# Layer 0's adaLN modulation as column-quarter products on TensorE

## The chip, the cores and the metric

One core of a Trainium2 chip runs the kernel. Its engines are TensorE (PE, with its weight loads listed as PEld), VectorE (DVE), ScalarE (ACT), GpSimd (POOL) and SyncE (SP), whose queue issues the large loads. Each has an instruction stream of its own, in a fixed order; semaphores make one wait for another. The metric is the device time of the kernel in microseconds, lower is better. "Span" is the time from the first to the last instruction of one profiled execution.

## The reference

A sequence of 256 tokens with 1024 features goes through a first block (gated delta rule and dilated attention side by side, then a convolved, gated FFN) and a second block of two layers (attention and a mixture of 16 experts), whose norms are modulated by a row computed from a conditioning vector `c`:

```python
x = x + jnp.concatenate([y_a, y_b], axis=-1) @ w_out     # first block: mix
x = x + (silu(conv(h @ w_gate)) * (h @ w_up)) @ w_down   # first block: FFN
for i in range(2):                                       # second block
    mod = silu(c) @ ada_w[i] + ada_b[i]                  # [1, 1024] @ [1024, 6144]
    sh1, sc1, g1, sh2, sc2, g2 = split(mod, 6)
    x = x + g1 * mixer(rms_norm(x) * (1 + sc1) + sh1)
    x = x + g2 * moe(rms_norm(x) * (1 + sc2) + sh2)
```

The change touches `mod` for i = 0, which depends on `c` alone. It is computed while the first block runs, long before layer 0 needs it.

## The kernel before

All weights are streamed once from HBM through SBUF, mostly in units of 1 MB ([128, 2048] fp32), issued by SP into a ring of rooms (`w`, four of them; the modulation's units into `wa`, two rooms). Large products with 256 tokens split each fp32 operand into a high and a low half (`wh`, `wl`; `hh`, `hl`; `yh`, `yl`) and make three products of them (lines L543 and L559 to L561); a split is a cast on ACT and a subtraction on DVE, or on POOL for a part of the units (L232). PSUM has two rings of four tiles, tag `pa` for the projections and `pb` for everything else; a projection to token rows (`tok`) holds two `pa` tiles while its products add up, the output projection (`mix`) one for each token block and half of the columns.

The first block runs in these stages: features of the delta rule (L543, `pa`), convolved on DVE (L798); decay factors and heads (L835 to L903); the inverse of a triangular matrix by doubling (levels: two products on 64x64 blocks at L917, then R copied by DVE at L927, then Y and X updated at L933 and L934); joining of the halves (L942, L948); the chunk recurrence (L959); dilated attention (L604 to L627); the output projection (L559 to L561 with `yh`, `yl`); the norm (L441 products that only keep PE busy, L473, transposes L481); and the FFN (L543 with `pb`).

The second block's modulation is worked in between. `ada(n)` issues the next n units, with fractions carried; 48 units make both layers. In the delta rule `fill(n, more)` advances a "filler" (the projections `w_v`, `w_z` and the dilated attention) by n steps and calls `ada(more)` at each; the remaining units are issued in the FFN's loop. A unit, before, is half of the 1024 rows (four blocks of 128) of 512 columns. `ada_unit` multiplies each block of 128 rows by its 128 values of silu(c), one per partition (`csil`), and adds it up in `acc` [128, 512]: three blocks on DVE (L376 for the first of all, L381 for the others), the fourth scaled on ACT (L378) and added on POOL (L379). After two units the column's eight blocks are in `acc`, and `ada_sum` adds up the 128 partitions on PE: four products of `ones` with 128 columns each (L393), on four different parts of 32 columns of the array. For the gates g1 and g2 a product with the identity adds the bias (L396). ACT copies the result (L398) and sends it to a row in DRAM, `adar` (L399), from which the second block reads it.

The program's text gives only a first order: a scheduler with a priority by program order places each instruction where the tiles it needs are free, so it decides where the modulation's instructions stand on each engine.

Of the kernel before, what the change touches and what calls it, by code (L numbers as in the profile page):

```python
# [27 lines left out]
# columns of the packed per-partition parameters  # L28
# [7 lines left out]
# columns of the packed rows that every partition gets  # L36
ROW = {"alog": (0, 4), "dtb": (4, 8), "rb": (8, 24), "lam": (24, 280)}
NROW = 280
# columns of the shape constants
# [7 lines left out]
# the first block needs those up to here  # L47
# [3 lines left out]
def _constants():  # L51
# [23 lines left out]
    # negated bias of the merged dilated attention: [q, head, (previous block | own block) keys back to front]  # L75
# [8 lines left out]
    # one-hot T5 bucket of rel = key - query, for rel = 127 .. -384  # L84
# [9 lines left out]
def _pack(inp):  # L94
# [6 lines left out]
    def feat(w):  # L101
        """[D, n] -> units of two blocks of 128 columns, each [128, k, 128 columns]"""
        n = w.shape[1]
        return A(w.reshape(KD, 128, n // 256, 2, 128).transpose(2, 1, 3, 0, 4)).reshape(n // 256, 128, 2048)

    def tok(w):
        """[D, n] -> units of 512 columns and half the rows, each [128, 4 k, 512 columns]"""
        n = w.shape[1]
        return A(w.reshape(2, 4, 128, n // 512, 512).transpose(3, 0, 2, 1, 4)).reshape(n // 256, 128, 2048)
# [27 lines left out]
    o["ada_w"] = A(g["ada_w_2"].reshape(2, 2, 4, 128, 12, 512).transpose(0, 4, 1, 3, 2, 5)).reshape(48, 128, 2048)  # L137
# [19 lines left out]
class InOrder:  # L157
    """an engine whose instructions keep their order in the program"""
# [10 lines left out]
def tile_block(ctx: ExitStack, tc: tile.TileContext, a: dict, out: bass.AP, dbg=None):  # L169
# [60 lines left out]
    def split(h, l, i, eng=None):  # L230
        """i = h + l exactly, each of a float32r's width"""
# [32 lines left out]
    # the tensor engine's clock rises while x is on its way  # L264
# [25 lines left out]
    def wpair(ap, n):  # L290
        """(e, i) -> the i-th 512 columns of a unit for one of two experts; the n-th unit of a layer also finds room where activations were"""
# [30 lines left out]
    def after(i, name):  # L322
        """i is issued behind an instruction of its engine"""
# [3 lines left out]
    # rooms for split halves: s of two tiles of their own, 8 of one where activations are not  # L327
# [10 lines left out]
    def subs(ap, w=None, pinned=False, by=None, behind=None):  # L338
        """a unit of weights, loaded now or already on its way, as two split halves"""
# [25 lines left out]
    def ada_unit(n):  # L365
        """half the rows (four blocks) of 512 columns of a layer's modulation, every fourth block on GpSimd"""
        l, s, u = n // 24, n // 2 % 12, n % 2
        w = adap.tile([128, 2048], F32, tag="wa", name="wa", bufs=2)
        nc.sync.dma_start(w, a["ada_w"][n])
# [16 lines left out]

    def ada_sum(l, s, acc):
        """sum over partitions; with the bias for the gates, which are used as rows"""
# [16 lines left out]
    def ada(n):  # L405
        """n units more, fractions carried"""
# [12 lines left out]
    def ada_finish(l, t):  # L419
        """shift and scale as columns (the gates, used as rows, have the bias already)"""  # L420
# [15 lines left out]
    def warm(*waits):  # L436
        """holds the tensor engine's clock up through waits; nothing reads the products"""
# [5 lines left out]
    def rsq(o, i, scale):  # L443
        """o = (i * scale + eps) ** -0.5 through the activation tables"""
# [10 lines left out]
    def norm_rows(update=None, column_major=False, between=None, scaled=True):  # L455
        """x after update(b, c) of its [block, half row] pieces, and the rows of x over their root mean square"""
# [19 lines left out]
    def turned(src, column_major=False):  # L476
        """[128 tokens, 2, D] -> (j, [128, 2 blocks of columns from j on, 256 tokens]) in PSUM"""
# [27 lines left out]
    def spread(rs):  # L505
        """[128, 256 tokens]: the factor of each token, on every partition"""
# [7 lines left out]
    def kept(r, n):  # L514
        """r, the clock held up while the first columns are made"""
        warm(*[r[:, 128 * (i % 2):128 * (i % 2) + 16] for i in range(n)])
        return r

    def cols_split(turned_, r, scale, bias):
        """rows turned before their factors r were known, as two split halves"""  # L520
# [16 lines left out]
    def feat(p, h, wh, wl):  # L537
        """p[128 features, 256 tokens]; wh, wl [128, 8 k, 128]"""
# [12 lines left out]
    def tok_half(p, u, h, k, k0=0):  # L551
        """adds blocks k .. k + 3 of the rows, a unit of [128, 4 k, 512], to p[b] [128 tokens, 512]; in two steps"""
# [12 lines left out]
    def tok(units, h, done):  # L565
        """[128 tokens, 512] for both token blocks; four steps, then done(p)"""
# [11 lines left out]
    def weave(*parts):  # L578
        """runs (generator, steps a round) side by side in program order"""
# [10 lines left out]
    def lag(n, *stages):  # L590
        """stage j of item i comes j steps after its first stage"""
# [7 lines left out]
    def scores(qT, kT, blk, half, nbias, pt, den):  # L599
        """pt [128, 384] gets exp(s - max): keys 0..255 of query block 1, then keys 0..127 of query block 0.  # L600
        q comes negated; nbias [128, 256] is the negated bias for the keys of the (previous | own) block, back to front."""
# [13 lines left out]
    def flip(pt):  # L615
        """[q, keys] probabilities -> [keys, 2 blocks, q]"""
# [12 lines left out]
    def plain_heads(h0, n, qT, kT, v, nbias, y):  # L629
        """heads h0 .. h0 + n - 1 of plain attention; y(pair) gives the places of a pair's output"""  # L630
# [24 lines left out]
    # ================= first block =================  # L655
# [69 lines left out]
    n = 0  # L725
# [985 lines left out]
```

## Time and profile before

| | |
|---|---|
| median of the runs shown | 1169.7 us (1168.49 to 1181.19) |
| span of the profiled execution | 1168.8 us |
| PE busy | 1091.2 us, 93% |
| DVE busy | 668.5 us, 57% |
| ACT busy | 467.4 us, 40% |
| POOL busy | 202.3 us, 17% |
| DMA | 349.75 MB, mean 299 GB/s |
| mean granted clock of TensorE | 0.980 of full speed |

The page gives each engine's busy time over the whole span; the windows view gives it for stretches, and the share of a stretch in which PE is not busy is what can be won there. The waits view adds up the idle time of an engine in front of its instructions by what released them. The timeline lists instructions by start, with the idle time before each in brackets. Rows of one kind that follow each other are put together and counted.

### The profile page before, as it was taken

The numbers are of one execution on the slowest core, as the hardware profiler recorded it, in microseconds if no ns is written. First come the engines' busy times: TensorE is split into PE (matmuls) and PEld (weight loads), VectorE is DVE, ScalarE is ACT, GpSimd is POOL, SyncE is SP. The second block draws the span as 40 slices with busy tenths as digits, with TensorE's granted clock in tenths as the row PEclk, the third lists the DMA queues.
The fourth block names the chain that finished last, engine by engine and source line by source line (L and its number), as shares of the span: only waits on it lengthen the run. The fifth ranks groups of instructions, "written<-read, shape, count | busy, mean of one in ns | idle before, by whom it ended". The sixth has DMA issues, their size and how long they took to land. (4 is left out here: it accounts for less than half of the span.)

```text
span 1168.8 us, 16805 instructions
## 1 busy us (share of the span) xinstructions
PE 1091.2 (93%) x6428; PEld 713.0 (61%) x6428; DVE 668.5 (57%) x1283; ACT 467.4 (40%) x942; POOL 202.3 (17%) x156
## 2 busy tenths in 40 slices
PE   8978889899999989999899998898999899999798
PEld 6957677788898868787334434236876544443332
DVE  6999987899999866777322212026656723221212
ACT  5763365655555565667211112016555511110200
POOL 2245543133123242001000000004221100000000
PEclk9999979899999999999999999899999989999999
DMA  8664766777877965356888999998653679899995
GB/s 323 253 252 182 264 246 223 284 285 279 338 284 311 369 247 177 135 200 221 333 349 343 418 422 423 406 421 316 191 184 144 254 305 372 327 424 424 422 419 203
DMA packets 53083, 349.75 MB, mean 299 GB/s; under 512 B 6392, under 2 KB 7192, under 8 KB 13056
## 3 DMA queue, kind: packets, MB, share of 16 engines
q1 hardware_dynamic: 50288, 342.51, 75.2%
q0 software_dynamic: 1792, 5.62, 1.7%
q8 instruction: 55, 0.90, 0.3%
q10 hardware_dynamic: 912, 0.43, 0.1%
q14 instruction: 36, 0.29, 0.1%
HBM read 347.40 MB, written 1.14 MB: 298 GB/s over the span
## 5 line engine op out<-in xcount | busy, mean ns | idle before, releaser
L1544 PE MATMUL pb<-w,XT 128*64 128x512 f32 x864 | 200.1, 609 | 10.3 <-PEq L1504 10.3
L232 DVE TENSOR_TENSOR wl<-w,wh 128x1024 fp32r<-128x1024 f32 x110 | 141.7, 1292 | 40.5 <-ACT wh L232 34.8
L232 ACT CAST wh<-w 128x1024 fp32r<-128x1024 f32 x132 | 137.6, 1044 | 65.5 <-PE pa L560 45.9
L1544 PEld LDWEIGHTS pb<-w,XT 128*64 128x64 f32 x864 | 61.9, 140 | 128.2 <-issue 124.5
L379 POOL TENSOR_TENSOR acc<-acc,wa 128x512 f32<-128x512 f32 x48 | 78.1, 1627 | 204.1 <-DVE acc L381 132.9
L1563 DVE TENSOR_TENSOR he<-he,pb 128x512 f32<-128x512 f32 (+1 forms) x20 | 11.4, 580 | 175.7 <-PE pb L1544 175.7
L381 DVE SCALAR_TENSOR_TENSOR acc<-wa,csil,acc 128x512 f32<-128x512 f32 x120 | 104.0, 867 | 13.4 <-POOL acc L379 8.9
L1581 PE MATMUL pb<-w,heT 128*64 128x512 f32 x480 | 108.1, 597 | 1.5 <-ACT heT L222 1.5
L1562 ACT ACTIVATE he<-pb 128x512 f32<-128x512 f32 (+1 forms) x20 | 10.0, 512 | 209.3 <-PE pb L1544 209.3
L559 PE MATMUL pa<-wh,hh 128*128 128x512 f32 x224 | 91.0, 408 | 2.5 <-ACT hh L532 2.5
L560 PE MATMUL pa<-wh,hl 128*128 128x512 f32 x224 | 88.4, 395 | 3.0 <-POOL hl L530 1.7
L561 PE MATMUL pa<-wl,hh 128*128 128x512 f32 x224 | 88.4, 394 | 0.0
L232 POOL TENSOR_TENSOR wl<-w,wh 128x1024 fp32r<-128x1024 f32 x22 | 54.7, 2488 | 178.3 <-ACT wh L232 139.4
L1584 DVE SCALAR_TENSOR_TENSOR he<-pb,gsl,g 128x512 f32<-128x512 f32 x32 | 24.0, 751 | 96.9 <-PE pb L1581 96.8
L1581 PEld LDWEIGHTS pb<-w,heT 128*64 128x64 f32 x480 | 32.8, 137 | 64.6 <-issue 58.5
L543 PE MATMUL pb<-hh,whl 128*128 128x256 f32 x320 | 62.3, 288 | 0.9 <-DVE gate L1076 0.9
L232 ACT CAST yh<-he 128x512 fp32r<-128x512 f32 x30 | 18.5, 616 | 103.6 <-DVE he L1584 103.6
L378 ACT ACTIVATE wa<-wa,csil 128x512 f32<-128x512 f32 x48 | 34.6, 722 | 58.5 <-DMA wa<-in_ada_w 57.2
L543 PE MATMUL pb<-hh,wh 128*128 128x256 f32 x192 | 55.5, 289 | 1.1 <-DVE hl L236 1.1
L543 PE MATMUL pb<-hl,wh 128*128 128x256 f32 x192 | 55.4, 288 | 0.0
L543 PE MATMUL pb<-hh,wl 128*128 128x256 f32 x192 | 55.2, 288 | 0.0
L543 PEld LDWEIGHTS pb<-hh,whl 128*128 128x128 f32 x320 | 51.3, 192 | 4.0 <-issue 3.4
(455 smaller groups left out, 2352.4 us busy)
## 6 DMA issues: line engine op xcount, KB each, us to landing
w<-in_m_gu SPq DMA_DIRECT2D x108, 1024.0 KB
w<-in_m_dn SPq DMA_DIRECT2D x58, 1024.0 KB
wa<-in_ada_w SPq DMA_DIRECT2D x48, 1024.0 KB
w<-in_w_gu SPq DMA_DIRECT2D x22, 1024.0 KB
w<-in_a_qkv SPq DMA_DIRECT2D x12, 1024.0 KB
wx<-in_m_gu SPq DMA_DIRECT2D x12, 1024.0 KB
w<-in_b_qkv SPq DMA_DIRECT2D x12, 1024.0 KB
w<-in_w_dn SPq DMA_DIRECT2D x11, 1024.0 KB
```

Of the source, the lines that this page charges most:

```text
L232: return A_.copy(h, i), (eng or V).tensor_tensor(l, i, h.bitcast(F32), op=ALU.subtract)
L378: A_.activation(wi, wi, AF.Copy, scale=csil[:, k:k + 1])
L379: G.tensor_tensor(acc, acc, wi, op=ALU.add)
L381: V.scalar_tensor_tensor(acc, wi, csil[:, k:k + 1], acc, op0=ALU.mult, op1=ALU.add)
L543: mm(p, w[:, c], r[:, k, :], start=(n == 0), stop=(n == 3 * KD - 1))
L559: mm(p[b], hh_, wh[:, c], start=(k == k0), stop=False)
L560: mm(p[b], hl_, wh[:, c], start=False, stop=False)
L561: mm(p[b], hh_, wl[:, c], start=False, stop=((k + 1) % KD == k0))
L1544: mm(pu[i][64 * e:64 * e + 64, :], xt[k // 4][:, k % 4, c0 + 64 * e:c0 + 64 * e + 64], w(e, i), start=(k == 0), stop=(k == KD - 1))
L1563: V.tensor_tensor(he[:, cs], he[:, cs], pu[1][:, cs], op=ALU.mult)
L1581: pin(mm(pd[h][64 * e:64 * e + 64, :], heT[:, k, e, :], w(e, i), start=(k == 0), stop=(k == 3)))
L1584: V.scalar_tensor_tensor(he, pd[h], gsl, g2[:, h * 512:(h + 1) * 512], op0=ALU.mult, op1=ALU.mult)
```

## The change

For layer 0 the weights are packed in 24 units of another shape: unit 8 s + k holds the 128 rows of block k and 2048 columns, the s-th third of the 6144. Layer 1's 24 units stay in the old form. `ada_unit(n)` sends units below 24 to a new function, `ada_rows(s, k)`: it loads the unit and makes four products, one for each quarter of 512 columns, with `csil` of block k as the stationary operand (repeated to 32 columns), each into its own 32 partitions of one PSUM tile of the ring `pa`. The tile adds up over k = 0 to 7, so it is held for eight units. Behind the last unit of a third that has a gate's columns, eight products with the identity add the bias; then one copy on ACT and one DMA send 2048 columns to `adar`. For layer 0 there are no multiplications on DVE, ACT or POOL any more, and no `ada_sum`. The rest of the difference is comments and docstrings left out, which shifts the line numbers: L543 becomes L570, L559 to L561 become L586 to L588, L604 and L605 become L631 and L632, L917 becomes L944, L927 becomes L954, L933 and L934 become L960 and L961, L959 becomes L986.

```diff
-    o["ada_w"] = A(g["ada_w_2"].reshape(2, 2, 4, 128, 12, 512).transpose(0, 4, 1, 3, 2, 5)).reshape(48, 128, 2048)
+    o["ada_p"] = A(g["ada_w_2"][0].reshape(8, 128, 3, 2048).transpose(2, 0, 1, 3)).reshape(24, 128, 2048)
+    o["ada_w"] = A(g["ada_w_2"][1].reshape(2, 4, 128, 12, 512).transpose(3, 0, 2, 1, 4)).reshape(24, 128, 2048)
...
     def ada_unit(n):
+        if n < 24:
+            return ada_rows(n // 8, n % 8)
         l, s, u = n // 24, n // 2 % 12, n % 2
         w = adap.tile([128, 2048], F32, tag="wa", name="wa", bufs=2)
-        nc.sync.dma_start(w, a["ada_w"][n])
+        nc.sync.dma_start(w, a["ada_w"][n - 24])
...
+    def ada_rows(s, k):
+        w = adap.tile([128, 2048], F32, tag="wa", name="wa", bufs=2)
+        nc.sync.dma_start(w, a["ada_p"][8 * s + k])
+        if k == 0:
+            ada_acc[0] = ps(512, "pa")
+        p = ada_acc[0]
+        for j in range(4):
+            mm(p[32 * j:32 * j + 32, :], csil[:, k:k + 1].to_broadcast([128, 32]), w[:, j * 512:(j + 1) * 512],
+               start=(k == 0), stop=(k == KD - 1 and (4 * s + j) // 2 not in (2, 5)))
+        if k < KD - 1:
+            return
+        for c in range(4):
+            for j in range(4):
+                if (4 * s + j) // 2 in (2, 5):
+                    n = 16 * s + 4 * j + c
+                    mm(p[32 * j:32 * j + 32, c * 128:(c + 1) * 128], P("adab")[:, n:n + 1].to_broadcast([128, 32]), ident,
+                       start=False, stop=(c == 3))
+        sb = adap.tile([128, 512], F32, tag="acc", name="adarow", bufs=3)
+        A_.copy(sb, p)
+        nc.scalar.dma_start(adar[0][s * 2048:(s + 1) * 2048].rearrange("(j c) -> j c", j=4),
+                            sb.rearrange("(j r) c -> j r c", j=4)[:, 0, :])
```

How the scheduler places them is seen in the order of the two programs. First DVE, in two levels of the inverse (R, Y and X are the level's; `acc` and `wa` the modulation's; `wl` a split of a projection's weights). Before:

```order
L927 COPY R<-pb 128x512
L376 TENSOR_SCALAR acc<-wa,csil 128x512
L381 SCALAR_TENSOR_TENSOR acc<-wa,csil,acc 128x512 x2
L232 TENSOR_TENSOR wl<-w,wh 128x1024
L933 TENSOR_TENSOR Y<-Y,pb 128x512
L934 TENSOR_TENSOR X<-X,pb 128x512
L381 SCALAR_TENSOR_TENSOR acc<-wa,csil,acc 128x512 x3
L232 TENSOR_TENSOR wl<-w,wh 128x1024
L927 COPY R<-pb 128x512
```

The same levels now:

```order
L954 COPY R<-pb 128x512
L234 TENSOR_TENSOR wl<-w,wh 128x1024
L960 TENSOR_TENSOR Y<-Y,pb 128x512
L961 TENSOR_TENSOR X<-X,pb 128x512
L234 TENSOR_TENSOR wl<-w,wh 128x1024
L954 COPY R<-pb 128x512
```

The six modulation passes of a level are gone from DVE; its own instructions and the splits follow each other directly. On PE, at the end of the inverse and the start of the chunk recurrence (`kb`, `qb` are the dilated attention's heads), before:

```order
L942 MATMUL pb<-Y,ax 64x64 x8
L604 MATMUL pb<-kb,qb 128x256
L605 MATMUL pb<-kb,qb 128x128
L948 MATMUL pb<-R,X 64x64 x8
L604 MATMUL pb<-kb,qb 128x256
L605 MATMUL pb<-kb,qb 128x128
L959 MATMUL pb<-vbt,YF 128x128 x4
```

The same place now:

```order
L399 MATMUL pa<-wa,csil 32x512 x4
L407 MATMUL pa<-ident,prm 32x128 x8
L969 MATMUL pb<-Y,ax 64x64 x8
L631 MATMUL pb<-kb,qb 128x256
L632 MATMUL pb<-kb,qb 128x128
L975 MATMUL pb<-R,X 64x64 x7
L399 MATMUL pa<-wa,csil 32x512 x4
L975 MATMUL pb<-R,X 64x64
L631 MATMUL pb<-kb,qb 128x256
L632 MATMUL pb<-kb,qb 128x128
L986 MATMUL pb<-vbt,YF 128x128 x4
```

The second third's last unit and its bias now stand in front of L969, and the third third's first unit within the chain of L975. Third, PE from the end of the output projection to the FFN's first product, before:

```order
L561 MATMUL pa<-wl,yh 128x512
L441 MATMUL pa<-ident,x 16x384 x4
L481 MATMUL pb<-ident,xn 128x128 x16
L543 MATMUL pb<-hh,wh 128x256
L543 MATMUL pb<-hl,wh 128x256
```

And now:

```order
L588 MATMUL pa<-wl,yh 128x512
L399 MATMUL pa<-wa,csil 32x512
L468 MATMUL pa<-ident,x 16x384 x4
L508 MATMUL pb<-ident,xn 128x128 x16
L399 MATMUL pa<-wa,csil 32x512 x7
L407 MATMUL pa<-ident,prm 32x128 x8
L570 MATMUL pb<-hh,wh 128x256
```

The last two units of layer 0 and their bias stand around the norm, seven of their eight products between the last transposes and the FFN. Units 16 to 23 are placed in pieces of 4, 4, 5, 3, 1 products up to the output projection and 4, 3, 1, 7 from there on.

## Rows read from the trace of the kernel before

**Rows 1.** The page, busy times over the whole span.
```profile
PE 1091.2 (93%) x6428; PEld 713.0 (61%) x6428; DVE 668.5 (57%) x1283; ACT 467.4 (40%) x942; POOL 202.3 (17%) x156
```

**Rows 2.** Windows: width, busy us (instructions) by engine, granted clock, DMA share, GB/s.
```profile
43.00:59.80 16.80, 14.58 (x119) 14.18 (x118) 16.77 (x24) 12.00 (x18) 6.93 (x4) 1.00 0.59 199
59.80:94.06 34.26, 27.59 (x184) 21.84 (x184) 32.52 (x64) 21.58 (x37) 14.39 (x10) 1.00 0.55 211
94.06:150.16 56.10, 47.36 (x682) 38.54 (x682) 52.99 (x57) 19.16 (x28) 30.16 (x17) 1.00 0.71 256
150.16:188.60 38.44, 35.77 (x203) 27.23 (x204) 29.05 (x91) 22.74 (x70) 15.18 (x17) 0.82 0.67 226
188.60:219.71 31.11, 26.58 (x121) 19.41 (x119) 26.58 (x37) 15.40 (x29) 10.72 (x7) 0.96 0.80 318
219.71:424.80 205.09, 201.57 (x1497) 181.31 (x1497) 181.38 (x240) 109.55 (x176) 52.11 (x34) 0.99 0.80 305
```

**Rows 3.** The same windows, instructions of the modulation's weight tile `wa` alone.
```profile
43.00:59.80 16.80, 6.37 (x6) 1.45 (x2) 2.01 (x2) 1.00 0.59 199
...
94.06:150.16 56.10, 30.25 (x27) 5.79 (x8) 13.81 (x9) 1.00 0.71 256
```

**Rows 4.** Waits of PE, 43 to 220 us: total, times, longest, us.
```profile
PE pb L917 <- DVE R L927: 4.5, 3, 1.9
PE pa L543 <- DVE wl L232: 3.1, 2, 1.6
...
PE pb L835 <- ACT sq L833: 2.3, 2, 1.6
...
PE pb L884 <- DVE t5v L856: 1.8, 1, 1.8
...
PE pb L884 <- DVE kq L840: 1.1, 1, 1.1
```

**Rows 5.** Timeline of PE, two experts' products: start, us, instruction, records.
```profile
599.23 1.46 PE L1544 MATMUL pb<-wx,XT 128*64 128x512 f32 x6
600.52 1.46 PE L1544 MATMUL pb<-w,XT 128*64 128x512 f32 x6
```

**Rows 6.** Timeline of PE at two sums of the modulation; [idle before <- releaser].
```profile
91.26 0.43 PE L393 MATMUL pb<-acc,ones 128*32 128x128 f32 x8
91.61 0.66 PE L903 MATMUL pb<-ident,kq 128*128 128x128 f32 x4
...
118.03 0.39 PE L561 MATMUL pa<-wl,hh 128*128 128x512 f32 x1
118.35 0.43 PE L393 MATMUL pb<-acc,ones 128*32 128x128 f32 x8
119.96 0.45 PE L917 MATMUL pb<-Y,os 64*64 64x64 f32 x8 [1.19 <-DVE Y L933]
```

**Rows 7.** Windows (first two rows) and timeline of PE in the chunk recurrence.
```profile
148.00:150.00 2.00, 1.25 (x28) 1.00 1.02 279
...
154.00:156.00 2.00, 1.25 (x4) 0.50 1.00 422
...
156.57 2.05 PE L959 MATMUL pb<-vbt,YF 128*128 128x128 f32 x8 [1.32 <-DVE YF L949]
...
170.40 1.16 PE L959 MATMUL pb<-v,aq 128*128 128x128 f32 x8 [0.67 <-ACT v L222]
```

**Rows 8.** Timeline of PE, end of the norm and start of the FFN.
```profile
217.01 1.64 PE L481 MATMUL pb<-ident,xn 128*128 128x128 f32 x8 [2.39 <-DVE xn L473]
219.71 0.58 PE L543 MATMUL pb<-hh,wh 128*128 128x256 f32 x1 [1.05 <-DVE hl L236]
```

**Rows 9.** ScalarE's waits for `wa`, 59 to 220 us; timelines of SP's queue, ScalarE.
```profile
ACT wa L378 <- DMA wa<-in_ada_w: 27.2, 10, 7.4
...
136.22 5.38 SPq L369 DMA_DIRECT2D wa<-in_ada_w  x2
...
142.45 0.72 ACT L378 ACTIVATE wa<-wa,csil 128x512 f32<-128x512 f32 x1 [7.35 <-DMA wa<-in_ada_w]
```

## The prediction

> **What bounds the kernel now.** I read the page's busy times first: TensorE (PE) is busy 93% of the span [rows 1], so what is saved on another engine helps only where PE waits for it, and what is added to PE costs its full length unless it falls into such a wait. So I cut the span into stages and asked for the busy time in each [rows 2]: 43 to 59.8 (the convolved features), 59.8 to 94.06 (decay factors, heads, first products), 94.06 to 150.16 (the doubling levels of the triangular inverse, with the projections `w_v` and `w_z` between), 150.16 to 188.6 (chunk recurrence and dilated attention), 188.6 to 219.71 (output projection and norm), and from there the FFN. The reader is to see the difference between a stage's width and its PE busy time: 2.2, 6.7, 8.7, 2.7 and 4.5 us, together 24.8 us of idle PE. That is all that relief of another engine can give before the FFN; in the FFN it is 3.5 of 205.1 us. In the first three stages VectorE (DVE) is busy 16.8 of 16.8, 32.5 of 34.3 and 53.0 of 56.1 us. How much of that the modulation holds stands in the same view taken for its weight tile `wa` [rows 3]: 6.4 us in the first stage, 30.3 in the third. And PE's waits [rows 4] are mostly for DVE: for R and Y of a level, and for wl, the low half of split weights. So DVE sets what PE waits for until about 150 us, and the modulation is more than half of its load in the levels.
>
> **The price of a unit.** Before, a 1 MB unit cost DVE three passes of 128x512, ScalarE one and GpSimd one, and every second unit four small sums on PE. After it, each of layer 0's 24 units costs four PE products of 32x512 (a wave: four different 32-column parts of the array), and nothing on DVE and GpSimd. The trace has no such product. The nearest is the experts' product of 512 columns in the same type, two side by side: from 599.23 to 600.52 six records took 1.29 us [rows 5]. A matmul leaves two records (the four of a sum are eight in [rows 6]), so a pair, four records, takes 0.86 us. Whether four go at once is shown by the sums: four different parts at 128 columns took 0.35 us from start to start [rows 6], where a quarter of 0.86 is 0.215; the other 0.13 is entering and leaving. I add 0.09 for the step from a full-width row into it (118.03 to 118.35 [rows 6], 0.32 us, where such rows follow each other by 0.23). A wave is 0.86 + 0.13 + 0.09, about 1.09 us. Ends: 0.86 (nothing lost) and 1.72 (two at a time); I take 1.09, since its nearest row has four parts at once.
>
> A rule of the Trainium skill speaks against four parts being worth four: in "TensorE: Matmul & The Clock Gate", section "Measured speedup vs the span model", three column tiles at N=512 gave 2.38 times, not three. The same loss per tile here would make a wave an estimated 1.16 us, and the sum below 1.9 us larger; no run here shows it yet.
>
> **What is added and what goes, on PE.** The order breaks the last third (units 16 to 23) into pieces, so 24 units become 27 waves: 29.4 us. Each of the two sets of bias (eight products of 128 columns on two parts, so 512 columns a part, as in a wave) is 1.09 too, 2.2 together. Gone are eight sums with two sets of bias before the FFN, and four with two in the FFN; a sum is 0.44 with its step in, a set of bias behind it 0.35 [rows 6]: 4.2 and 2.5 us.
>
> **The sum by stage** (waves and bias, less sums, less the waits that come back).
> First: no wave. PE's idle 2.2 us is for split halves on a DVE that never rests there and loses 6.4 of 16.8 us; 1.7 come back. -1.7.
> Second: six waves, +6.5; one sum, -0.4; of 6.7 us idle the three waits for DVE come back, wl 1.5, t5v 1.8 and kq 1.1 [rows 4], -4.4; those for ScalarE's squares, 2.3, stay. +1.7.
> Third: ten waves and a set of bias, +12.0; five sums and two sets, -2.9. Nearly all of the 8.7 us idle is for DVE, which loses 30.3 of 53.0 us; besides, the wave itself now stands in front of a level's product, where PE waited 1.19 us for Y [rows 6]. I leave 0.3 us for each of five levels: -7.2. +1.9.
> Fourth: six waves, +6.5; two sums, -0.9; the wait for YF, 1.3 [rows 7], nearly comes back, -1.2. And the clock: after a stretch in which PE was busy 1.25 of 2 us, the granted clock was 0.50, the 1.2 GHz level [rows 7]; eight records of L959 took 2.05 us there and 1.16 at full clock later, a ratio of 1.8. A mean clock of 0.82 over the stage's 38.44 us [rows 2] means 13.8 us at that level; less the wait, 12.5, of which 5.5 are lost. If DVE no longer opens gaps before it, the clock may hold; if the stage's own waits are the cause, nothing comes back. I count half, -2.7. +1.7.
> Fifth: two waves within the projection, +2.2. One ahead of the norm's warming products lies in the later wait of 2.39 us for xn [rows 8] and costs nothing (1.1 if that wait goes). Seven quarters (two waves) and the bias stand between the last transposes and the FFN's first product, +3.3. The accumulator holds one of four `pa` tiles through the projection, and a split half comes later: between nothing and two waits as long as the longest for wl, 1.6 each [rows 4]; I take 1.0, as the waves fill part of it. Back come the wait for hl, 1.05, and half of that for xn, 1.2 [rows 8]. +4.3.
> FFN: -2.5; PE is 98% busy there [rows 2], and layer 1's units stay as they were.
> Sum: -1.7 + 1.7 + 1.9 + 1.7 + 4.3 - 2.5 = +5.4 us. The profiled span becomes 1174.2; the median of the runs shown lies 0.9 above its own, so 1175.1.
>
> What ScalarE and GpSimd are freed of I count at nothing: PE's waits for ScalarE's squares have their cause in the products ahead of them, not in the modulation.
>
> **The rivals.**
> *All idle time and the clock come back.* PE's added work less the sums is 29.4 + 2.2 - 4.2 - 2.5 = 24.9 us, as much as its idle time before the FFN, 24.8; with the 5.5 us of clock the kernel gains 5.4: 1164.3. For it: waves and waits stand at the same places in the levels. Against: the squares and the norm's chain don't queue behind the modulation.
> *Slower: PE waits for the weight loads.* ScalarE waited ten times, 27.2 us in all and 7.4 at the longest, for `wa` [rows 9]. That held up only one later add; now the queue that waits is PE's own, in order, with the level's products, the projection and the FFN's first product behind it. For it: `wa` keeps its two rooms, and where the DMA engines are full at 422 GB/s [rows 7] each 1 MB of other weights ahead of it takes 2.5 us, as towards the FFN, with units 20 to 23. Against: loads issued from 136.22 on were in use at 142.45 [rows 9], 6.2 us, while a room is needed again two units later; ten units in the third stage's 56.1 us make that 11.2 us. It decides where a load takes longer than that from the release of its room, as with two more loads of 1 MB ahead of it than these had. If half of ScalarE's waits pass to PE: +13.6, 1189.
> *The waits don't come back.* If only half of the 16.7 us of waits that I count does, and nothing of the clock: 8.4 + 2.7 more, 1186. For it: a chain that has lost one wait often meets the next; against it [rows 2, 3], DVE's load.
> *No overlap.* If the quarters run one by one, 96 x 0.86 = 82.6 us stand in place of 29.4: +53, 1228. Against: [rows 6].
>
> **How the numbers follow.** The forecast as summed, from 1168 to 1181: 0.67. All back: 0.08. Load waits: 0.12. Waits not back: 0.10. No overlap: 0.03. What a measurement of this kernel can tell from no change is about 1%, 11.7 us, so 1158.0 to 1181.4. Faster than that needs all waits back and a wave cheaper than any row, 0.86, too (6.2 less, 1158): 0.03 with what I don't see. Slower: the last three rivals, less their mild ends: 0.23. Same: 0.74. The range goes from just below the first rival, 1163, to between the second and the third, 1188, which leaves out no more than 2 in 10.
>
> **What would show it.** In the profile after: a wave of eight records with about 1.1 us to the next row (1.7 or 3.4 would be wrong); `wa` gone from DVE and GpSimd before the FFN; PE's waits for R and Y in the levels under 0.5 us each; no PE wait for `wa`, or, if the slower rival holds, most of them at units 20 to 23. A granted clock of 1.00 near 154 to 165 would give another 2.7 us, a second fall takes as much. The levels should end, and the FFN begin, some 2 and 8 us later than now, and the FFN be 2 us shorter. The forecast is wrong if the FFN's start moves by less than 2 or more than 15 us.

## The result and the profile after

The changed kernel takes 1158.4 us in the median of its runs, 1157.08 to 1160.73; the ratio to the kernel before is 0.988, with a 95% interval of 0.9835 to 0.993. In a second series (e10) it was 0.990 (0.985 to 0.994). So it is about 11 us faster, where 1175.1 us, some 5 us slower, was forecast: it lies 4.6 us below the lower end of the range. The profiled execution has a span of 1158.7.

The page's busy times of the changed kernel:

```profile
PE 1103.9 (95%) x6524; PEld 710.5 (61%) x6524; DVE 595.2 (51%) x1211; ACT 449.6 (39%) x907; POOL 161.3 (14%) x132
```

TensorE is busy 12.7 us more than in [rows 1], and the span is 10.1 us shorter. The same stages as in [rows 2], cut at the same landmarks of the program: first product that sums up the squares (`sq`), first level product, joining of the halves, first transposes of the delta rule's output, first product of the FFN, first transposes behind it (columns as in [rows 2]):

```profile
43.00:58.17 15.17, 15.17 (x127) 14.20 (x126) 15.06 (x26) 11.99 (x16) 5.30 (x2) 1.00 0.47 154
58.17:89.36 31.19, 29.85 (x202) 21.24 (x199) 18.50 (x47) 16.52 (x30) 7.58 (x5) 1.00 0.79 299
89.36:146.53 57.17, 57.17 (x737) 41.48 (x736) 21.30 (x28) 13.04 (x16) 15.70 (x10) 1.00 0.74 271
146.53:180.69 34.16, 33.15 (x217) 22.14 (x215) 18.98 (x79) 19.04 (x63) 5.92 (x9) 1.00 0.69 236
180.69:215.72 35.03, 33.23 (x172) 21.66 (x171) 18.60 (x31) 14.10 (x25) 5.79 (x4) 1.00 0.71 259
215.72:412.61 196.89, 195.49 (x1452) 178.36 (x1450) 173.51 (x232) 108.37 (x172) 48.66 (x32) 1.00 0.84 316
```

Two things are to be seen. PE's idle time before the FFN (width less busy time, stage by stage) is 0, 1.3, 0, 1.0 and 1.8 us, together 4.1 where it was 24.8. And the granted clock is 1.00 in every stage, where the recurrence had 0.82 and the norm 0.96. By stage, with the landmarks of the two traces; a change is that of the stretch which ends at the landmark:

| from the landmark before to | before, us | after, us | change | forecast |
|---|---|---|---|---|
| first level product | 93.98 | 89.36 | -4.6 | 0.0 |
| joining of the halves | 150.16 | 146.53 | +1.0 | +1.9 |
| first transposes of the output | 188.57 | 180.69 | -4.3 | +1.7 |
| first product of the FFN | 219.71 | 215.72 | +3.9 | +4.3 |
| first transposes behind the FFN | 424.83 | 412.61 | -8.2 | -2.5 |
| the end | 1168.8 | 1158.7 | +2.1 | 0 |

What PE still waits for from 43 to 220 us is all in four rows, against [rows 4]:

```profile
PE pb L508 <- DVE xn L500: 1.4, 1, 1.4
PE pb L862 <- ACT sq L860: 1.3, 1, 1.3
PE pa L399 <- DMA wa<-in_ada_p: 0.9, 1, 0.9
PE pa L588 <- POOL wl L234: 0.3, 1, 0.3
```

No level waits for R or Y any more. The weight loads are waited for once, 0.9 us, at unit 16. A wave in PE's timeline:

```profile
114.29 0.39 PE L588 MATMUL pa<-wl,hh 128*128 128x512 f32 x1
114.61 1.06 PE L399 MATMUL pa<-wa,csil 128*32 128x512 f32 x8
115.61 1.15 PE L944 MATMUL pb<-Y,os 64*64 64x64 f32 x32
```

From 114.61 to 115.61 it takes 1.00 us, and the step into it 0.32 instead of 0.23, another 0.09: together the 1.09 of the forecast. The end of the norm and the start of the FFN, to be read beside [rows 8]:

```profile
211.98 1.09 PE L508 MATMUL pb<-ident,xn 128*128 128x128 f32 x8 [1.45 <-DVE xn L500]
213.00 1.92 PE L399 MATMUL pa<-wa,csil 128*32 128x512 f32 x14
214.75 1.04 PE L407 MATMUL pa<-ident,prm 128*32 128x128 f32 x16
215.72 0.39 PE L570 MATMUL pb<-hh,wh 128*128 128x256 f32 x1
```

The FFN's first product follows the bias without a wait, and takes 0.39 us where it took 0.58 at the half clock [rows 8].

### The profile page after: what moved, and what is told of

It reads as the page before. It is cut to its first block, busy times and chain, and to the rows that moved or that the text cites. A ratio compares the mean times of both kernels' runs of the same rounds, so it can differ in the third digit from the quotient of the medians.

```text
span 1158.7 us, 16795 instructions
## 1 busy us (share of the span) xinstructions
PE 1103.9 (95%) x6524; PEld 710.5 (61%) x6524; DVE 595.2 (51%) x1211; ACT 449.6 (39%) x907; POOL 161.3 (14%) x132
## 5 line engine op out<-in xcount | busy, mean ns | idle before, releaser
L1571 PE MATMUL pb<-w,XT 128*64 128x512 f32 x864 | 200.4, 613 | 10.1 <-PEq L1531 10.1
L234 DVE TENSOR_TENSOR wl<-w,wh 128x1024 fp32r<-128x1024 f32 x110 | 135.2, 1230 | 58.5 <-ACT wh L234 49.5
L586 PE MATMUL pa<-wh,hh 128*128 128x512 f32 x224 | 91.6, 410 | 2.5 <-ACT hh L559 2.5
L588 PE MATMUL pa<-wl,hh 128*128 128x512 f32 x224 | 89.3, 399 | 0.0
L570 PE MATMUL pb<-hh,whl 128*128 128x256 f32 x320 | 61.9, 286 | 0.0
L383 POOL TENSOR_TENSOR acc<-acc,wa 128x512 f32<-128x512 f32 x24 | 41.4, 1724 | 125.9 <-DVE acc L385 90.9
L570 PE MATMUL pb<-hh,wh 128*128 128x256 f32 x192 | 54.4, 284 | 0.0
L570 PE MATMUL pb<-hl,wh 128*128 128x256 f32 x192 | 54.3, 283 | 0.0
L570 PE MATMUL pb<-hh,wl 128*128 128x256 f32 x192 | 54.3, 283 | 0.0
L570 PEld LDWEIGHTS pb<-hh,whl 128*128 128x128 f32 x320 | 51.2, 191 | 2.3 <-issue 1.8
L587 PEld LDWEIGHTS pa<-wh,hl 128*128 128x128 f32 x224 | 43.3, 193 | 12.5 <-DVE hl L560 2.2
L586 PEld LDWEIGHTS pa<-wh,hh 128*128 128x128 f32 x224 | 42.8, 192 | 12.8 <-ACT hh L559 3.4
```

The costliest lines, as they stand in the source:

```text
L234: return A_.copy(h, i), (eng or V).tensor_tensor(l, i, h.bitcast(F32), op=ALU.subtract)
L383: G.tensor_tensor(acc, acc, wi, op=ALU.add)
L570: mm(p, w[:, c], r[:, k, :], start=(n == 0), stop=(n == 3 * KD - 1))
L586: mm(p[b], hh_, wh[:, c], start=(k == k0), stop=False)
L587: mm(p[b], hl_, wh[:, c], start=False, stop=False)
L588: mm(p[b], hh_, wl[:, c], start=False, stop=((k + 1) % KD == k0))
```

## The experiments

Two theories stood at first. **A**: VectorE's load made PE's waits, and the clock fell behind them; relief (taking the modulation's multiplications off VectorE, ScalarE and GpSimd) gives them back, and a wave costs its length. **B**: the waits are the chains' own, and what helped is that PE had something to do in them. In the stage rows below the columns are those of [rows 2], and the cuts are the landmarks of the table above. Ratios are to the kernel before.

**e1: relief without waves.**

```diff
# kernel before, ada_unit
         for i in range(4):
             wi, k = w[:, i * 512:(i + 1) * 512], 4 * u + i
+            if n < 24 and k:
+                continue
             if k == 0:
```

> The kernel before, with layer 0's multiplications left out but for the first block of each column group (12 passes on VectorE stay of 72, none on ScalarE and GpSimd); loads, sums and layer 1 stay. No product is added on TensorE. Theory A (the waits of TensorE before the FFN are VectorE's load, and the clock falls behind them): some 20 of 24.8 us of idle come back and 5 to 7.6 us of clock too, 1142 to 1149 us, granted clock 1.00 from 150 to 166. Rival B (the waits are the chains' own latency, and what helped was that TensorE had something to do in them): 1162 to 1168 us, waits for R and Y still over 5 us in all, the clock falls as before.

Measured: 1147.7 us, ratio 0.979 (0.971 to 0.987), 22 us less than before.

```profile
43.00:56.84 13.84, 13.84 (x118) 13.84 (x117) 13.78 (x24) 10.79 (x15) 5.28 (x2) 1.00 0.93 356
56.84:88.12 31.28, 26.48 (x169) 21.38 (x167) 21.73 (x50) 16.66 (x30) 7.31 (x5) 0.95 0.62 248
88.12:136.74 48.62, 48.62 (x698) 40.32 (x697) 25.21 (x35) 13.94 (x20) 13.79 (x8) 1.00 0.88 315
136.74:168.85 32.11, 29.91 (x202) 23.10 (x198) 20.93 (x84) 18.67 (x64) 8.14 (x12) 0.95 0.75 259
168.85:199.70 30.85, 27.56 (x127) 20.60 (x123) 17.68 (x28) 14.09 (x25) 5.80 (x4) 0.95 0.75 283
199.70:402.85 203.15, 200.45 (x1498) 180.89 (x1498) 172.77 (x235) 109.91 (x177) 51.75 (x32) 0.99 0.79 302
```

Theory A holds for the levels: without any wave in them PE is busy 48.62 of 48.62 us, so every wait there came from the modulation's multiplications. Their releasers in [rows 4] are VectorE's; what ScalarE's and GpSimd's share in it was, e1 does not show, since it takes all three away. The FFN starts 20.0 us earlier. But 4.8, 2.2 and 3.3 us of idle stay in the second, fourth and fifth stage, the clock still falls in these three (0.95), and the FFN is 203.15 us long, against 196.89 of the changed kernel, which has far more to do before it. In the second stage the waits for VectorE went, and one for ScalarE's squares of 4.1 us came in their place. Of the 24.8 us of idle time relief alone takes 14.5 back, the changed kernel 20.7.

**e2: the waves of two blocks alone.**

```diff
# changed kernel, ada_rows
-        for j in range(4):
+        for j in range(4 if k in (0, KD - 1) else 0):
```

> The changed kernel with the products of blocks 0 and 7 alone, so that 18 of 24 waves are left out; all loads stay. Theory A (TensorE is without idle time before the FFN, a wave costs its 1.0 us in full): 18 us less than the changed kernel's 1158.4, so about 1140 us. Rival B (the waves stand in waits that are there anyway and keep the clock up): not below 1153 us, with waits in the levels and a granted clock of 0.50 near 150 to 166.

Measured: 2083 us, which says nothing of the change: PE spends it on the kernel's second way through the experts, which the program keeps for an expert that gets more tokens than its 64 places, and waits there for weights. That the missing modulation changes the router's choice is the likely reason; it was not looked at.

```profile
PE pb L1275 <- DMA ow<-in_m_gu: 175.2, 63, 9.3
```

What can be read is the time before that, here the levels and the projection with the norm:

```profile
83.89:134.01 50.12, 50.12 (x682) 40.40 (x681) 23.62 (x31) 14.07 (x19) 15.02 (x9) 1.00 0.73 274
164.62:202.24 37.62, 30.72 (x148) 21.40 (x147) 22.23 (x34) 15.37 (x27) 8.81 (x6) 0.96 0.73 252
```

The levels have no idle time, and the clock holds up to the norm, against rival B. The FFN starts at 202.24, 13.5 us earlier than in the changed kernel, not 18: idle time took 5.1 us more in the projection and norm (6.9 instead of 1.8). So a wave costs less than its length near the norm.

**e3: waves without relief.**

```diff
# kernel before, ada_unit
+        if n < 24:
+            pd = ps(512, "pa")
+            for j in range(4):
+                mm(pd[32 * j:32 * j + 32, :], csil[:, 0:1].to_broadcast([128, 32]),
+                   ones[:, 0:1].to_broadcast([128, 512]), start=True, stop=True)
```

> The kernel before with all its work on VectorE, ScalarE and GpSimd, and besides for each of layer 0's units one wave of four 32x512 products of constants, whose result nobody reads (24 waves, 24 us of TensorE's work, with no wait for a weight load). Theory A (VectorE's load makes the waits, the waves alone don't shorten them): waves hide in the levels' waits, up to 8.7 us, the clock holds, 5 to 7.6 us, the rest is added: 1177 to 1184 us. Rival B (what helps is TensorE's work in the gaps, by the clock): below 1170 us. If the clock falls stay as they were: 1184 or more.

Measured: 1186.1 us, ratio 1.010 (1.002 to 1.018). The levels and the recurrence:

```profile
96.15:160.25 64.10, 59.52 (x777) 43.67 (x777) 48.42 (x58) 19.94 (x29) 29.86 (x18) 0.97 0.64 230
160.25:202.15 41.90, 41.90 (x233) 27.67 (x233) 28.03 (x94) 22.00 (x70) 13.31 (x16) 0.80 0.48 168
```

Theory B falls as the whole story, and theory A's 1177 to 1184 was missed where it counted on the clock; it is the case "if the clock falls stay". PE still idles 4.6 us in the levels, where VectorE has its old load, and the clock falls all the same: 0.80 in a stage in which PE is never idle, behind the levels' gaps. Waves alone did not hold the clock.

**e4, e5, e12: one third the old way.** Each puts one third of layer 0 back on VectorE, ScalarE and GpSimd.

```diff
# changed kernel, ada_unit, with layer 0's old packing beside the new one
-        if n < 24:
+        if n < 24 and n // 8 in (0, 1):      # e4;  (0, 2) in e5;  (1, 2) in e12
             return ada_rows(n // 8, n % 8)
```

> The changed kernel with the last third of layer 0 (units 16 to 23, columns 4096 on) multiplied the old way. Takes 11 waves and a bias set off TensorE before the FFN, gives four sums with two bias sets and 24 passes to VectorE. Theory A (the wave is dear once no wait is left, and VectorE has room from 147 us on, where it is busy 41 of 69 us): 9.6 us less of TensorE's work, some 4.4 us of waits and up to 2 us of clock back: about 1155 us, 3 less than the changed kernel. Rival B (VectorE's queue holds TensorE up there as before): 1160 us or more.

> The changed kernel with the middle third (units 8 to 15, which fall into the levels) multiplied the old way. Takes eight waves and a bias set off TensorE (9 us), gives four sums with two bias sets (2.6). Theory A (VectorE's load in the levels makes waits and the clock fall behind them): most of the 8.7 us of the levels' waits and 5 us of clock return, 1164 to 1167 us. Rival C (a wave's price decides, VectorE has room for eight units): 1150 to 1154 us, levels still without idle time.

> The changed kernel with the first third (units 0 to 7, from the features to the first levels) multiplied the old way. Takes eight waves off TensorE (8 us), gives four sums (1.8). Theory A: waits for wl, t5v and kq come back, 4 to 7 us, no fall of the clock: 1156 to 1160 us. Rival D (any block of units on VectorE costs more than its waves, as e4 and e5 showed for the other thirds): 1162 to 1166 us.

Measured: e4 1165.6 us (0.996, 0.993 to 1.000), e5 1164.2 (0.994, 0.992 to 0.997), e12 1165.5 (0.995, 0.992 to 0.998). Each third undone costs 5 to 7 us of the 11 (against e10's 1159.1), so the three aren't additive: about half of the gain is lost with any of them. e4, recurrence, projection and FFN:

```profile
146.93:180.81 33.88, 29.81 (x186) 23.17 (x185) 28.35 (x90) 22.59 (x69) 11.04 (x13) 0.95 0.51 169
180.81:213.42 32.61, 27.22 (x122) 20.17 (x121) 21.29 (x35) 14.68 (x27) 9.28 (x6) 0.94 0.93 340
213.42:416.83 203.41, 201.68 (x1498) 181.62 (x1498) 178.07 (x240) 109.10 (x177) 50.74 (x34) 0.98 0.80 307
```

The waves gone from these two stages shorten them by 2.7 us only: PE idles 9.5 us in them instead of 2.8, and the clock falls again. The FFN is 6.5 us longer. e5 falls in the levels:

```profile
89.29:144.55 55.26, 52.13 (x690) 42.46 (x689) 40.22 (x47) 17.84 (x24) 22.08 (x14) 0.94 0.67 249
```

with one wait of 3.1 us for R and the clock at 0.94; the recurrence behind it pays more, 5.8 us over the changed kernel's, with the clock at 0.87:

```profile
144.55:184.54 39.99, 37.19 (x217) 25.31 (x213) 24.80 (x88) 19.78 (x64) 12.24 (x14) 0.87 0.61 205
```

e12 has the first two stages of the kernel before back, nearly to the row:

```profile
43.00:59.25 16.25, 14.03 (x114) 13.63 (x114) 16.21 (x23) 11.58 (x17) 6.78 (x4) 1.00 0.60 204
59.25:93.60 34.35, 27.66 (x183) 21.91 (x182) 32.62 (x64) 21.47 (x37) 14.48 (x10) 1.00 0.55 211
```

with 2.2 and 6.7 us of idle. My expectation for e4 was that of the wave's price (1155 us), and it was wrong; for e12 it was 1156 to 1160, too low as well. Rival D, that any block of units on VectorE costs more than the waves it saves, is what the three thirds show where the units of one follow each other. e5 came out at the lower edge of theory A.

**e6, e7, e9: the old form spread thin.** The old third's units are issued in turn with the others.

```diff
# changed kernel as in e4, ada
-            ada_unit(ada_next[0])
+            ada_unit(seq[ada_next[0]])
# e6: seq = 0, 1, 16, 2, 3, 17, ... 14, 15, 23;  e7: 8, 0, 9, 10, 1, 11, ... (thirds 1 and 2 the old way)
# e9: units 16 to 23 at places 1, 3, 6, 8, 11, 13, 16, 18
```

> The changed kernel with the last third multiplied the old way, as in e4, but its eight units issued in turn with the others (two units as waves, one the old way), so VectorE never has more than a third of the old load. Theory A (waits grow out of a full VectorE; at a third of the load few return): 8 waves and a bias set less, 2.6 us of sums more, 2 to 4 us of waits: 1152 to 1156 us. Rival D (any multiplication on VectorE and GpSimd brings waits and clock falls back, as e4 did): 1160 to 1166 us.

> The same with only the first third as waves and the other two the old way, issued in turn (old, wave, old). Theory A: 16 waves and two bias sets less on TensorE, 5.2 us of sums more; with two thirds of the old load VectorE is near full in the levels again, 8 to 12 us of waits and 4 of clock return: 1156 to 1162 us. Rival D: 1165 us or more. If TensorE's price alone counted: 1146.

> As e6 (the last third the old way, in turn with the others), but its eight units at places 1, 3, 6, 8, 11, 13, 16 and 18 of 24, so that VectorE is done with them before the output projection and the last waves stand around the norm as in the changed kernel. Theory E (in e6 the FFN gave back what the stages before it had gained, since two old units and the gap at the norm fell into it): the FFN's start stays near e6's 208 us and the FFN is 198 to 201 us long again: 1151 to 1155 us, below the changed kernel. Rival D (half of the old load on VectorE while it lasts brings waits and clock falls back in the levels): 1158 us or more.

Measured: e6 1159.5 us (0.990, 0.983 to 0.996), the same as the changed kernel; e7 1173.1 (1.001, 0.997 to 1.005), no better than before; e9 1164.2 (0.995, 0.992 to 0.998). e6 is the one to look at. Its FFN starts at 208.21, 7.5 us before the changed kernel's, with no clock fall up to there and 5.4 us of idle time (4.1 in the changed kernel), as theory A had it. Then the FFN gives it all back:

```profile
208.21:412.94 204.73, 199.81 (x1490) 179.96 (x1490) 170.96 (x234) 109.58 (x177) 51.84 (x33) 0.99 0.80 302
```

It is 7.8 us longer than 196.89, and 3.5 of it stand in one row of PE's waits:

```profile
PE pa L1089 <- ACT mh L234: 3.5, 2, 2.7
```

Some 2.5 us, by the prediction's prices, are the four sums and two sets of bias that are in this FFN again. e9 tested whether it was the two old units left in e6's FFN: theory E falls, since without their multiplications the FFN is still 203.8 us long (two sums and two sets of bias, 1.6 us, stay in it), and the second stage and the recurrence lost some 2 us each too (32.8 and 35.7 us long, against 30.7 and 33.3 in e6). For e6 and e7 theory A had expected less than came, 1152 to 1156 and 1156 to 1162. e7 is as rival D had it (1165 us or more); e6 lies between the two and just below rival D's 1160. So a third of the old load costs 5 to 7 us in one piece, 5 when it is crowded towards the front (e9), and nothing that these runs can tell when every third unit is an old one (e6).

**e8: every wave twice.**

```diff
# changed kernel, ada_rows
+        pd = ps(512)
+        for j in range(4):
+            mm(pd[32 * j:32 * j + 32, :], csil[:, k:k + 1].to_broadcast([128, 32]), w[:, j * 512:(j + 1) * 512],
+               start=True, stop=True)
```

> The changed kernel with each unit's four products made a second time into a tile that nobody reads: 24 waves more, 24 us by the trace's 1.0 us each. Theory A (TensorE has 4 us of idle left before the FFN, so a wave now costs its length): 1180 to 1184 us. Rival B (waves still lie in waits): under 1172 us. If the products of one wave didn't overlap, 0.86 each, more than 1230.

Measured: 1183.4 us, ratio 1.011 (1.008 to 1.014): 24 us for 24 more waves, 1.0 each, as theory A said. The four products of a wave overlap. Two waves in a row:

```profile
56.89 1.06 PE L400 MATMUL pb<-wa,csil 128*32 128x512 f32 x8
57.78 1.04 PE L403 MATMUL pa<-wa,csil 128*32 128x512 f32 x8
58.75 0.70 PE L866 MATMUL pb<-sq,ones 128*128 128x512 f32 x1
```

The first takes 0.89 us to the start of the second, so where PE has no idle time left a further wave costs its length of 0.9. The rest of the 1.0 need not be the waves': the last waves and a set of bias now stand in the FFN, and the clock is at 0.50 for 6.9 us around its start, as in e11 below.

**e10: the changed kernel again**, beside e9, e11 and e12.

> The changed kernel itself, beside the others on the same chip: 1158 us, ratio 0.988 to 0.992.

Measured: 1159.1 us, 0.990 (0.985 to 0.994). Its FFN is 197.4 us long.

**e11, e13: the waves at the norm.** e11 holds the waves of units 22 and 23 and their bias back behind the first features of the FFN; e13 does the same and puts five products that nobody reads in their place.

```diff
# changed kernel, ada_rows (e11 and e13); first_ff is the last feature product of f = 0
+            if 8 * s + k >= 22:
+                after(o, first_ff[0])
# e13 (and e14 on the kernel before): to_cols_split, behind the transposes
+        if not behind and rooted:
+            warm(*[xn[:, 1, c:c + 16] for c in (0, 200, 400, 600, 800)])
```

> The changed kernel with the waves of its last two units (22 and 23) and their bias held back behind the first feature products of the FFN. TensorE's work is the same. Theory F (the seven quarters and the bias between the last transposes and the FFN are a cover, they fill the norm's waits and hold the clock): PE waits for hl again, 1 us, and the granted clock falls to 0.50 at the FFN's start for about 6.8 us: 1160 to 1163 us, the FFN 3 to 6 us longer than the changed kernel's 196.9 and its start 2 to 3 earlier. Rival G (they cost their length wherever they stand): 1157 to 1159 us, no fall of the clock.

> As e11 (waves of units 22 and 23 held back into the FFN), and in their old place, between the last transposes and the FFN's first product, five products of 384 columns that nobody reads (0.64 us each by the norm's rows of the same form, 3.2 in all). Theory F (what e11 lost is the cover: the gap at the norm makes the clock fall): no granted clock of 0.50 at the FFN's start, the FFN about 201 us long (the changed kernel's 197 and 4.1 of waves moved into it), its start near 216: 1161 to 1163 us, less than e11's 1165.7 although TensorE has 3.2 us more to do. Rival G (e11 lost by something else in the FFN, such as the accumulator held there): 1166 to 1169 us.

Measured: e11 1165.7 us (0.995, 0.993 to 0.998), 6.6 more than e10 at equal work. PE's waits and its windows there (us, busy, granted clock, DMA):

```profile
PE pb L511 <- DVE xn L503: 2.2, 1, 2.2
PE pb L573 <- DVE hl L238: 1.6, 1, 1.6
```

```profile
210.00:214.00 4.00, 1.62 (x10) 0.76 0.69 238
214.00:218.00 4.00, 4.00 (x21) 0.50 0.06 25
```

PE was busy 1.62 of 4 us, the clock went to 0.50 and stayed there while the FFN began. The FFN starts 2.2 us earlier (213.47) and is 7.4 us longer (204.32). e13 has 3.2 us more for PE to do, and is not slower: 1164.3 us (0.995, 0.994 to 0.997). With its unread products the norm looks like this, and the FFN is 200.3 us long:

```profile
212.20 3.40 PE L471 MATMUL pa<-ident,xn 128*16 128x384 f32 x10
215.53 0.38 PE L576 MATMUL pb<-hh,wh 128*128 128x256 f32 x1
```

```profile
214.00:218.00 4.00, 4.00 (x25) 1.00 0.18 76
```

So the waves between the transposes and the FFN, which I had booked as 3.3 us of cost, are a cover: they stand where PE would wait 1.6 us for hl, and with something in that place, be it waves or unread products, the clock holds through the FFN's start. Theory F holds for the FFN; the total is 1.3 us above its upper edge, and 5.2 above e10, of which 4.1 are the waves and the bias that went into the FFN.

**e14: the cover in the kernel before.** The edit is e13's second one.

> The kernel before with the same five unread products between the last transposes and the FFN's first product. Theory F: they fill the wait for hl (1.05 us) and delay the FFN's first product by some 2.1, and if they hold the clock the FFN is 2 to 3 us shorter: 1168 to 1170 us, no change. If the clock falls in the wait for xn ahead of them (2.39 us), they can't hold it and run at half of it: 1172 to 1175 us. In neither case does cover at the norm alone explain the changed kernel's 1158.

Measured: 1171.4 us, ratio 1.001 (0.999 to 1.003). The projection and norm, and the FFN:

```profile
188.19:220.99 32.80, 29.29 (x131) 19.93 (x129) 27.85 (x40) 16.11 (x30) 10.72 (x7) 1.00 0.80 310
220.99:421.95 200.96, 198.96 (x1498) 179.18 (x1497) 179.49 (x237) 108.67 (x175) 56.27 (x34) 1.00 0.82 311
```

The fall at the FFN's start is gone and the FFN is 4.2 us shorter than in [rows 2], at a price of 1.3 in its start; 2.9 us are won by 422 us, and in the whole they don't show; in the profiled execution the clock is at half for 37.5 us behind that, against 27.4 before. Cover alone explains a part of the FFN's gain, not the 11 us.

**e15: the same at the next norm.**

```diff
# changed kernel, first norm of the second block
-    h = cols_split(tx, spread(rs[:, 2:4]), mod[0]["gs1"], mod[0]["sh1"])
+    h = cols_split(tx, kept(spread(rs[:, 2:4]), 4), mod[0]["gs1"], mod[0]["sh1"])
```

> The changed kernel with four unread products of 384 columns behind the second block's first norm (2.6 us, in waits of 1.8 and 1.0 us for the rows of the norm), where the granted clock still falls to 0.50 for 6.8 us at 420. Theory F carried over: the fall is gone or shorter, 1155 to 1158 us. Rival: the fall comes from the waits ahead of these products, 1159 to 1161 us, and 0.50 at 420 as before.

Measured: 1158.0 us, ratio 0.989 (0.988 to 0.991), against 0.988 and 0.990 of the changed kernel: no difference that these runs can tell. The fall itself is gone; the same window of e15 and, below, of the changed kernel:

```profile
424.00:428.00 4.00, 4.00 (x19) 1.00 0.61 242
```

```profile
424.00:428.00 4.00, 4.00 (x10) 0.50 0.59 238
```

No kernel of these was faster than the changed one by more than they can tell.

## Why the prediction was wrong, point by point

**The price of a wave: right.** 1.09 us with its step, as forecast; the ends of 0.86 and 1.72 and the rival without overlap fall with e8. The Trainium skill's measured speedup ("TensorE: Matmul & The Clock Gate", section "Measured speedup vs the span model"), carried on to four parts, had given an estimated 1.16 us; the trace's 1.00 us, 1.09 with the step, is below that. Waves and bias add up to 30.6 us here (25 groups in PE's timeline, 28.4 from their starts to the next rows without the waits behind them, and 0.09 each); 31.6 were forecast.

**The idle time: the step that failed first.** "I leave 0.3 us for each of five levels", "those for ScalarE's squares, 2.3, stay", half of the wait for xn, and the FFN's idle time left as it was: I took 16.7 us back and added 1.0 for PSUM and splits. In fact 20.7 came back before the FFN (24.8 to 4.1) and 2.1 in it (3.5 to 1.4). e1 shows why for the levels: their waits were the modulation's entirely, so nothing was to be left. Elsewhere relief alone left 10.3 us of idle (e1), and the changed kernel, whose waves the scheduler placed where PE would wait, has 6 less. The 1.0 for the held `pa` tile shows as a wait of 0.3 for a split.

**The clock: the second step.** "I count half, -2.7" for the fall in the recurrence, and the one at the FFN's start I didn't count. Both are gone: windows of 4 us add up to 13.6 us at half clock from 152 on and 6.9 from 216 on before, and none in the changed kernel up to 412. By the ratio of 1.8, less the idle time in them, these are some 7.5 us and not 2.7. PE's busy time up to the FFN tells the same: it grew by 16.7 us, with 30.6 of waves and bias added and 4.2 of sums removed, so 9.7 us of old work became shorter; the clock before the FFN explains some 5.5 of these, the other 4 I can't place. e1 and e3 show that neither relief nor waves alone keep the clock: with relief alone it fell in three stages, with waves alone to 0.80. With relief and six waves (e2) it fell only at the norm.

**The FFN: the third.** -2.5 was the sums alone. The other 5.7 us are the clock at its start (about 2), the idle time that went (2.1) and 1.6 that I can't place. e11, e13 and e14 show that the gap at the norm is behind the first two: 7.4 us are lost in the FFN when the last waves and a bias leave the norm (4.1 of them because they now stand in it), 4.2 are won in the kernel before by covering it.

**"+3.3" in the fifth stage** was about right as a length (2.7 from 213.00 to 215.72; the stage grew by 3.9, 4.3 were forecast) and wrong as a cost: e11.

**The signs.** By the prediction the levels were to end some 2 and the FFN to begin some 8 us later, and the FFN to be 2 us shorter. They came 3.6 and 4.0 us earlier, and the FFN is 8.2 us shorter. The forecast had even the direction wrong.

**The rivals.** The first one was right in its mechanism, nearly all idle time and the clock back, and I gave it 0.08. I had argued against it that the squares and the norm don't queue behind the modulation; in part the waves did what relief could not. It stopped at 1164.3 since it left out the FFN's clock and idle time. The wait for the loads came once, 0.9 us, and not at units 20 to 23. Waits that don't come back: none.

**What is given back later.** 12.2 us were won by the first transposes behind the FFN, 10.1 at the end. From there on the clock is at half for 37.5 us in the changed kernel's profiled execution and for 27.4 in that of before, both by windows of 4 us. In e10's execution of the changed kernel it is 31.2, and from the first transposes behind the FFN to the end it takes 743.0 us, where the kernel before took 744.0 and the first execution 746.1. So what is given back differs from one execution to the next, and isn't shown to come from the change. e15 took one such fall away without a measurable gain. Why they differ is open.

**What stays open.** Why the FFN is 200 to 206 us long in every variant with some of layer 0 in the old form, beyond the sums. PE's waits for ScalarE's `mh` are longer in e6 and e9 (3.5 and 1.8 us), but in e12 they are no longer than in e10 (1.1 each), so they are not the whole, and what holds `mh` was not separated. Nor was the part that freeing GpSimd and ScalarE has in the relief, which the prediction put at nothing.

## What to carry to other kernels

Where one engine is busy all through a stage and TensorE waits for it, all of TensorE's waits there can come back when that load goes, as in the levels (8.7 us of 8.7), unless the next engine takes its place, as the squares did in the second stage (4.8 of 6.7 us stayed in e1). Then ask what the clock does when the gaps close. What stays of the old load should be spread: a third in one piece lost about half of the gain, and so did one crowded towards the front (e9); as every third unit (e6) it lost none that these runs can tell. Independent small products are dear in a stage that is full (0.9 to 1.0 us each here); in the gap in front of the next full stage 3.2 us of them cost nothing that these runs can tell (e13 against e11), so look where a scheduler puts them before booking their length. A stage that follows such a gap belongs to the sum, even where the change takes hardly anything from it.

## What the runs showed of the hardware

Four products on four parts of 32 columns, 512 columns each and with four different moving operands, take 1.00 us from start to the start of the next other product, and 0.89 to that of another such four (e8), where one pair takes 0.86 [rows 5]; if one alone takes as long as a pair, the 1.00 us are 3.4 times as fast as one after another. The granted clock went to 0.50 around a stretch in which PE was busy 1.6 of 4 us (e11). It can be low in a stage that is full of work, behind gaps in the one before (e3: a mean of 0.80 over 41.9 us without an idle microsecond). With unread products of 3.2 us in the gap at the norm it stayed at 1.00 (e13, e14).
